# Loading the rows of three image pairs as bf16 with a casting DMA, in a convolution with max pooling

## The chip, the cores and the metric

The kernel runs on one core of a Trainium2 chip. A core has a matrix engine (TensorE, "PE" in the profile), three engines that work elementwise (VectorE or "DVE", ScalarE or "ACT", GpSimd or "POOL") and a synchronisation engine ("SP") that here only issues transfers. Each engine runs its own list of instructions in order; semaphores tie the lists together. SBUF is the core's working memory. PSUM, eight banks of 128 x 512 float32 here, takes the matrix engine's results; DVE and ACT read and write it, POOL does not in this kernel.

The metric is the time of one execution on the device in microseconds (us), the median of several runs. The times within a trace are counted from the start of its span.

## What is computed

A 3 x 3 convolution of 16 images with 64 channels of 64 x 64 to 128 channels, with a border of zeros, followed by the maximum over every 2 x 2 block:

```python
batch, c_in, h, w, c_out, k = 16, 64, 64, 64, 128, 3
x_pad = np.pad(x, ((0, 0), (0, 0), (pad, pad), (pad, pad)), mode='constant')
conv[b, co] += weight[co, ci, kh, kw] * x_pad[b, ci, kh:kh+h, kw:kw+w]   # for all b, co, ci, kh, kw
output[b, c, i, j] = np.max(conv[b, c, 2*i:2*i+2, 2*j:2*j+2])
```

Input and output are float32; the products are made in bf16 and summed in float32.

## The kernel before

**Tiling.** Two images form a pair: their 2 x 64 channels fill the 128 partitions, image 0 in the lower and image 1 in the upper half. A pair is cut into four quarters of 16 rows (R = 8 rows of the pooled result). There are eight pairs, so 32 steps, numbered 0 to 31. A step makes, for each of its two images l = 0 and 1, two banks: bank A and bank B, which together stand for the even and the odd rows of the convolution. A product is three matrix multiplications (one for each column of the 3 x 3 window) of 64 channels by 8 rows x 64 columns; the two images' products run side by side on the two halves of the array.

**Two kinds of steps.** The string SEQ gives each step a kind. The eight "K" steps (pairs 0 and 1) multiply the rows themselves, five products for an image. The 24 "W" steps (pairs 2 to 7, four steps each) save one: the vertical part of the window is rewritten so that four products are enough, at the price of sums and differences of rows that other engines make first. For a W step s these are:

- E.s: difference of neighbouring rows (128 x 512 elements), read by product P2
- S.s: sum of neighbouring rows (128 x 512), read by product P1
- V.s: difference of rows two apart (128 x 1024), read by P0 and P3; in a few steps made as two halves Ve.s and Vo.s

Each is written as bf16 (tiles we, ws, wv, vh) from rows that lie in SBUF as float32 (tiles wx). K steps have a similar sum, KS.s (tile ks), of rows that are bf16 already (tiles kx).

**Who makes them.** The suffix in the written order names the engine: `:v` DVE, `:g` POOL. POOL makes all V of the later steps and part of E and S. DVE makes the rest. The helper row_op (L195 to L200) issues them, and keeps note of the last one that DVE made through it (last_row): the next one on POOL waits for that one by a semaphore. For eleven steps a copy "CP.s:bank" (function lift, L287) first brings one of the two row operands into a PSUM bank, on ACT. Then DVE's E.s and S.s read one operand from PSUM and one from SBUF (two_rows, L294), and are not noted in last_row.

**Loads.** W rows come by SP's queue, one DMA for each quarter (LX.s, L262), with a row of overlap, into one of four float32 tiles wx (pair p uses wx[p % 4]; each has a zero row at top and bottom that POOL clears at the start, L150 to L152). Each such load waits until step s - 12 is finished (function paced). K rows of the later steps come by POOL's queue with a cast to bf16 (LK.s, L275).

**After the products.** ACT moves bank A to SBUF (EV, L429) and copies it as a start value into bank B (SE, L445; three of them on DVE, L443); DVE takes the larger of the two rows in bank B (MX, L449); ACT copies the odd columns out (OD, L472), DVE takes the larger of the columns (CM, L481), and SP stores the result (ST, L504). A bank is free for the next step's product or copy after EV or CM.

**The order.** The string ORDER (L16 to L80) lists every operation of every engine by hand; each engine works through its own entries in that order. A name such as P2.25.1:7 is product P2 of step 25, image 1, into bank 7. Entries that the change touches stand among these lines (L46 to L70). For POOL and DVE, the entries of steps 17 to 31 that matter here come in this order (CP on ACT and LX left out): S.16:v, V.16:g, S.15:g, E.17:v, E.19:g, S.17:v, V.17:g, S.19:g, E.22:v, S.22:v, V.22:g, KS.23:v, LK.27, E.20:v, V.19:g, E.21:g, V.20:g, S.20:v, V.21:g, S.21:g, E.24:g, V.24:g, S.24:v, KS.27:v, E.26:g, V.25:g, E.25:v, S.25:v, V.26:g, E.29:g, S.26:g, S.29:g, E.28:v, V.28:g, V.29:g, Ve.30:g, Ve.31:g, Vo.30:g, E.31:g, S.28:v, E.30:v, S.30:v, Vo.31:g, S.31:g.

Of the kernel before, what the change touches and what calls it, by code (L numbers as in the profile page):

```python
# [42 lines left out]
LX.19 OD.11.0 MX.12.0 P3.13.1 PBa.14.0:7 EV.13.1 LX.20 P2.13.0:6 P0.12.1 LX.22 CM.11.0 PBb.14.0  # L43
P2.15.1:0 S.16:v SE.13.0:2 MX.13.1 EV.12.1 SE.15.1:5 LK.23 P3.12.1 P1.12.0 OD.12.0 MX.14.0 ST.6
MX.12.1 P1.13.1 P0.13.0 OD.13.1 ST.2 P3.13.0 P0.15.1 CM.12.0 CM.13.1 EV.13.0 P3.15.1 P2.16.0:3
MX.13.0 EV.15.1 PR.14.0 PBa.14.1:6 CP.17:1 V.16:g S.15:g P1.13.0 P1.12.1 MX.15.1 SE.16.0:0 OD.14.0  # L46
E.17:v E.19:g CM.14.0 S.17:v OD.12.1 ST.4 OD.13.0 CM.12.1 P0.16.0 PBb.14.1 MX.14.1 V.17:g EV.16.0
ST.7 ST.9 P2.15.0:7 P1.15.1 LX.21 OD.15.1 P3.16.0 P2.16.1:1 S.19:g SE.15.0:3 P0.15.0 PR.14.1 CM.15.1
CM.13.0 CP.22:4 SE.16.1:5 OD.14.1 MX.16.0 P3.15.0 P2.17.1:2 P1.16.0 P0.16.1 EV.15.0 SE.17.1:7 E.22:v
OD.16.0 CM.14.1 MX.15.0 EV.16.1 P2.17.0:6 P3.16.1 P0.17.1 P1.15.0 SE.17.0:1 S.22:v CM.16.0 LX.24  # L50
P3.17.1 PAa.18.0:4 V.22:g PAa.18.1:0 P0.17.0 OD.15.0 MX.16.1 KS.23:v P1.16.1 PAb.18.0 EV.17.1 LK.27
CM.15.0 CP.20:2 P3.17.0 PBa.18.1:3 EV.17.0 MX.17.1 E.20:v OD.16.1 MX.17.0 V.19:g PAb.18.1 PBa.18.0:6
EV.18.0 P2.19.0:4 PBb.18.1 E.21:g EV.18.1 V.20:g P1.17.0 P1.17.1 ST.8 LX.26 CM.16.1 SE.19.0:5
MX.18.1 S.20:v OD.17.0 CM.17.0 P2.19.1:0 PBb.18.0 OD.17.1 SE.19.1:2 MX.18.0 P0.19.0 PR.18.1 OD.18.1
P2.22.1:1 P3.19.0 P0.19.1 PR.18.0 EV.19.0 CM.17.1 SE.22.1:7 OD.18.0 ST.11 P3.19.1 P2.20.0:4 EV.19.1
# [3 lines left out]
CM.22.1 EV.21.0 EV.21.1 MX.21.0 P3.21.1 P2.22.0:4 MX.21.1 SE.22.0:2 P1.20.0 P2.20.1:7 P2.24.1:0  # L59
P1.21.0 LX.29 ST.14 ST.12 OD.20.0 SE.20.1:6 CM.20.0 OD.21.0 CM.21.0 P0.22.0 P1.21.1 SE.24.1:3 ST.13  # L60
S.24:v EV.22.0 P0.20.1 P3.22.0 OD.21.1 KS.27:v CM.21.1 EV.20.1 P0.24.1 PAa.23.0:1 MX.22.0 E.26:g
P2.24.0:4 P3.24.1 EV.24.1 CP.25:7 V.25:g MX.24.1 PAb.23.0 PAa.23.1:5 SE.24.0:0 P1.22.0 P3.20.1
E.25:v EV.23.0 P1.24.1 P0.24.0 OD.24.1 S.25:v EV.24.0 P2.25.1:1 P3.24.0 MX.20.1 P2.25.0:7 PAb.23.1
LX.31 ST.17 P1.20.1 PBa.23.0:4 CM.24.1 OD.22.0 MX.24.0 SE.25.1:3 CM.22.0 EV.23.1 V.26:g SEv.25.0:2
P1.24.0 P0.25.1 OD.20.1 OD.24.0 EV.25.1 LX.30 ST.18 ST.22 ST.19 ST.21 PBb.23.0 P2.26.1:5 CM.20.1
ST.20 CM.24.0 ST.24 MX.23.0 SE.26.1:6 P3.25.1 P0.25.0 P3.25.0 PBa.23.1:0 EV.25.0 PR.23.0 P0.26.1
MX.25.1 P2.26.0:1 PBb.23.1 MX.25.0 E.29:g CP.28:7 S.26:g S.29:g E.28:v OD.23.0 P3.26.1 P1.25.0
V.28:g V.29:g CM.23.0 MX.23.1 Ve.30:g EV.26.1 P1.25.1 PAa.27.0:5 SE.26.0:4 PR.23.1 P0.26.0 MX.26.1
Ve.31:g P3.26.0 P1.26.1 Vo.30:g E.31:g OD.25.0 OD.25.1 EV.26.0 CM.25.0 S.28:v PAa.27.1:2 PAb.27.0
CP.30:7 CM.25.1 ST.25 MX.26.0 OD.23.1 P2.28.1:1 PBa.27.0:3 OD.26.1 PAb.27.1 P1.26.0 EV.27.0 CM.23.1  # L70
ST.23 PBb.27.0 PBa.27.1:0 CM.26.1 E.30:v SE.28.1:5 S.30:v Vo.31:g P0.28.1 P2.29.0:6 MX.27.0
P2.28.0:7 PBb.27.1 PR.27.0 P3.28.1 EV.27.1 OD.26.0 CM.26.0 ST.26 SE.29.0:2 MX.27.1 EV.28.1 OD.27.0
P2.29.1:4 P0.29.0 P3.29.0 PR.27.1 SE.28.0:1 EV.29.0 CM.27.0 MX.28.1 P0.28.0 P2.30.1:3 MX.29.0
# [10 lines left out]
def kernel(  # L84
# [14 lines left out]
    B, CI, H, W = x.shape  # L99
# [4 lines left out]
    R = HO // NQ  # L104
# [3 lines left out]
    const = ctx.enter_context(tc.tile_pool(name="const", bufs=1))  # L108
# [28 lines left out]

    def chunk(s):

        p, q = place[s]  # L140
        same = any(place[t] == (p, q - 1) and SEQ[t] == SEQ[s] for t in range(N))
        lo = 2 * R * q + 1 if same else max(0, 2 * R * q - 1)
        return p, lo, min(H, 2 * R * (q + 1) + 1)

    def half(s):
        return 2 * R * place[s][1] + R + 1

    NWX = 4
    wx = [const.tile([128, H + 2, W], FP32, name=f"wx_{i}") for i in range(NWX)]
    for t in wx:  # L150
        nc.gpsimd.memset(t[:, 0, :], 0.0)
        nc.gpsimd.memset(t[:, H + 1, :], 0.0)  # L152
    kx = {}

    def kx_of(p):
        if p not in kx:
            kx[p] = kx_pool.tile([128, H, W], BF16, name="kx")
        return kx[p]
# [10 lines left out]
    make_identity(nc, ident)  # L169
    zeros = const.tile([128, 512], BF16)  # L170
    begun = nc.gpsimd.memset(zeros, 0.0)
    wv = wraw.rearrange("a (c k) -> a k c", k=K * K)

    def ring(t, k):
# [20 lines left out]
    def row_op(e, out, in0, in1, op):  # L195
        inst = eng[e].tensor_tensor(out=out, in0=in0, in1=in1, op=op)  # L196
        if e == "g":
            behind(inst, last_row[0])
        else:
            last_row[0] = inst  # L200
# [50 lines left out]
    def paced(s, inst):  # L251

        for l in (0, 1):
            behind(inst, done.get((s - AHEAD[SEQ[s]], l)))
        if SEQ[s] == "K" and s < AHEAD["K"] and s not in kf:
            behind(inst, done["head"])

    def load(s, part, e):
        p, lo, hi = chunk(s)
        if SEQ[s] == "W":  # L260
            t = wx[p % NWX]
            paced(s, nc.sync.dma_start(out=t[:, lo + 1 : hi + 1, :], in_=rows_of(p, lo, hi)))  # L262
            return
        if s not in kf:
            kf[s] = const.tile([128, hi - lo, W], FP32, name=f"kf_{s}")
        a, b = {"": (lo, hi), "a": (lo, half(s)), "b": (half(s), hi)}[part]
        q = nc.scalar if e == "a" else nc.sync
        inst = q.dma_start(out=kf[s][:, a - lo : b - lo, :], in_=rows_of(p, a, b))
        paced(s, inst)
        if e == "a":  # L270
            behind(inst, begun)
# [15 lines left out]
    def lift(s, bank):  # L287

        lifted[s] = acc[bank]
        nc.scalar.copy(out=acc[bank], in_=wrow(s, 0))  # L290

    def two_rows(s, t, e, op):
        if e == "v" and s in lifted:
            nc.vector.tensor_tensor(out=t, in0=lifted[s], in1=wrow(s, 1), op=op)  # L294
        else:
            row_op(e, t, wrow(s, 0), wrow(s, 1), op)

    def wrow(s, a):

        p, q = place[s]  # L300
        f = 2 * R * q + a + 1
        return wx[p % NWX][:, f : f + 2 * R - 1 : 2, :]

    def ks(s, e):
        p, q = place[s]
# [8 lines left out]
    def rs_add(s):  # L314
# [23 lines left out]
    def rv(s, e):  # L338
        p, q = place[s]
        t = row["V", s] = v_pool.tile([128, 2 * R, W], BF16, name="wv")  # L340
        f = 2 * R * q
        u = wx[p % NWX]
        row_op(e, t, u[:, f + 2 : f + 2 + 2 * R, :], u[:, f : f + 2 * R, :], SUB)

    def rv_half(s, e, odd):

        p, q = place[s]
        t = row["V" + "eo"[odd], s] = vh_pool.tile([128, R, W], BF16, name="vh")
        f = 2 * R * q + odd
        u = wx[p % NWX]  # L350
        row_op(e, t, u[:, f + 2 : f + 1 + 2 * R : 2, :], u[:, f : f + 2 * R - 1 : 2, :], SUB)


# [168 lines left out]
    for token in ORDER.split():  # L522
        what, _, at = token.partition(":")
        name, *args = what.split(".")
        if name in PRODUCTS:
            s, l = int(args[0]), int(args[1][0])
# [87 lines left out]
```

## Time and profile before

| what | value |
|---|---|
| median of 3 runs | 103.27 us (103.05 to 103.55) |
| span of the profiled execution | 101.5 us |
| DMA packets | 13789, 24.07 MB |
| read from and written to HBM | 17.07 MB, 8.39 MB |

The page states the span of the profiled execution, from its first to its last instruction, and no total for it; the runs' times also hold what lies before and after the span.

How to read the rows: "L196" is line 196 of the kernel. A group names line, engine, operation, tile written and tiles read, their sizes (partitions x elements, type) and the number of instructions, then busy time, mean duration in ns, and the engine's idle time just before them with what ended it. Since one helper line makes many operations, the tile's name tells which: we, ws, wv, vh for E, S, V and the halves of V. "PEld" is the loading of weights. An engine's idle time costs something only where the engine is late for another.

The page's share of busy time in 40 equal slices of the span, in tenths:

```profile
PE   6999999999999999999989999999999999999950
...
DVE  0599999999999999799999989998999999888980
ACT  5599999999988999998999989989989889899840
POOL 7000898988598599989999999998599999999000
...
DMA  2999999991079989889998999999953915302353
```

All four computing engines are busy most of the time from about 10 us on.

### The profile page before, as it was taken

How to read it: one execution, taken by the hardware profiler on the slowest of the kernel's cores; microseconds unless marked ns; L12 is line 12 of the kernel's file. 1: busy time of each engine (PE TensorE's matmuls, PEld its weight loads, DVE VectorE, ACT ScalarE, POOL GpSimd, SP SyncE). 2: the span in 40 equal slices, each digit the busy share in tenths (PEclk: the TensorE clock that was granted, in tenths of full speed). 3: DMA queues.
4: the chain of work that ended last, by engine and by line, in shares of the span. 5: the costliest groups of instructions: out<-in, count | busy, mean ns of one | idle time of the engine just before them, and what ended most of it. 6: DMA issues, size and time to landing. Idle time of an engine off the chain costs nothing.

```text
span 101.5 us, 2486 instructions
## 1 busy us (share of the span) xinstructions
PE 96.4 (95%) x870; PEld 55.6 (55%) x870; DVE 91.4 (90%) x181; ACT 89.5 (88%) x198; POOL 79.3 (78%) x65
## 2 busy tenths in 40 slices
PE   6999999999999999999989999999999999999950
PEld 2356885466666666555645555455475555655510
DVE  0599999999999999799999989998999999888980
ACT  5599999999988999998999989989989889899840
POOL 7000898988598599989999999998599999999000
PEclk9999999999999999999999999999999999999999
DMA  2999999991079989889998999999953915302353
GB/s 45 328 248 403 417 376 337 326 226 33 6 203 390 233 166 302 315 222 291 273 329 260 261 237 311 374 392 308 295 222 122 344 58 201 108 29 78 110 189 121
DMA packets 13789, 24.07 MB, mean 237 GB/s; under 512 B 1104, under 2 KB 9680, under 8 KB 13776
## 3 DMA queue, kind: packets, MB, share of 16 engines
q1 hardware_dynamic: 12624, 22.16, 64.9%
q0 software_dynamic: 864, 1.56, 10.2%
q10 hardware_dynamic: 288, 0.20, 0.6%
q8 instruction: 7, 0.11, 0.4%
q14 instruction: 6, 0.05, 0.1%
HBM read 17.07 MB, written 8.39 MB: 251 GB/s over the span
## 4 chain that ended last, share of the span: by engine, by line
PE 83%; ACT 6%; DVE 3%; DMA 3%; issue 2%; DVEq 0%; ACTq 0%
PE acc L414 80%; DMA wraw<-in_weight_dram 3%; ACT acc L445 3%; PE acc L229 2%; DVE acc L449 2%; ACT od L472 2%; ACT ev L429 1%; DVE o L481 1%; ACT wq L191 1%; DVE acc L443 0%; PE acc L439 0%; DVEq L609 0%; DVEq L449 0%; DVEq L443 0%; ACTq L290 0%
## 5 line engine op out<-in xcount | busy, mean ns | idle before, releaser
L414 PEld LDWEIGHTS <-wt 64*128 64x128 bf16 x840 | 52.8, 94 | 37.3 <-issue 2.5
L414 PE MATMUL acc<-wv,wt 64*128 64x504 bf16 (+1 forms) x228 | 49.5, 377 | 0.3 <-ACT acc L445 0.3
L449 DVE TENSOR_TENSOR acc<-acc,ev 128x512 f32<-128x512 f32 x64 | 42.9, 693 | 2.0 <-ACT ev L429 1.1
L196 POOL TENSOR_TENSOR wv<-wx 128x1024 bf16<-128x1024 f32 x18 | 42.3, 2362 | 2.5 <-DVE ks L196 1.6
L414 PE MATMUL acc<-kx,wt 64*128 64x504 bf16 (+6 forms) x216 | 38.9, 350 | 0.0
L414 PE MATMUL acc<-ws,wt 64*128 64x512 bf16 (+1 forms) x144 | 35.2, 377 | 0.2 <-DVE acc L449 0.2
L414 PE MATMUL acc<-we,wt 64*128 64x512 bf16 (+1 forms) x144 | 35.1, 377 | 0.0
L429 ACT ACTIVATE ev<-acc 128x512 f32<-128x512 f32 x48 | 28.6, 610 | 1.1 <-PE acc L414 1.0
L445 ACT COPY acc<-acc 128x512 f32<-128x512 f32 x45 | 26.3, 588 | 2.0 <-PE acc L414 0.4
L481 DVE TENSOR_TENSOR o<-acc,od 128x256 f32<-128x256 f32 (+1 forms) x65 | 25.7, 412 | 1.4 <-ACT od L472 0.5
L472 ACT COPY od<-acc 128x256 f32<-128x256 f32 x64 | 23.6, 382 | 2.7 <-PE acc L414 1.9
L196 POOL TENSOR_TENSOR we<-wx 128x512 bf16<-128x512 f32 x11 | 14.0, 1272 | 2.8 <-DVE ks L196 1.7
L414 PE MATMUL acc<-ks,wt 64*128 64x504 bf16 (+1 forms) x48 | 12.5, 377 | 0.0
L414 PE MATMUL acc<-vh,wt 64*128 64x504 bf16 (+1 forms) x60 | 10.4, 376 | 0.0
L196 POOL TENSOR_TENSOR ws<-wx 128x512 bf16<-128x512 f32 x8 | 10.1, 1268 | 0.1
L275 POOL DMA_DIRECT2D kx<-in_x_dram x6 | 3.5, 590 | 8.0 <-ACT ev L429 8.0
L431 ACT COPY ev<-acc 128x512 f32<-128x512 f32 x16 | 9.3, 598 | 0.4 <-PE acc L414 0.3
L196 POOL TENSOR_TENSOR vh<-wx 128x512 bf16<-128x512 f32 x7 | 8.8, 1272 | 0.5 <-DVE ks L196 0.4
L294 DVE TENSOR_TENSOR we<-acc,wx 128x512 bf16<-128x512 f32 x11 | 7.5, 682 | 0.0
L294 DVE TENSOR_TENSOR ws<-acc,wx 128x512 bf16<-128x512 f32 x11 | 7.5, 681 | 0.0
L290 ACT COPY acc<-wx 128x512 f32<-128x512 f32 x11 | 6.7, 607 | 0.1
L509 PE MATMUL acc<-const-bfloat16-1.0 128*128 128x512 bf16 x8 | 3.6, 625 | 0.8 <-PEq L595 0.8
(30 smaller groups left out, 34.3 us busy)
## 6 DMA issues: line engine op xcount, KB each, us to landing
out_dram<-o SPq DMA_DIRECT2D x30, 256.0 KB, 5.8
wx<-in_x_dram SPq DMA_DIRECT2D x12, 512.0 KB, 6.3
wx<-in_x_dram SPq DMA_DIRECT2D x6, 544.0 KB, 6.5
wx<-in_x_dram SPq DMA_DIRECT2D x6, 480.0 KB, 6.7
kx<-in_x_dram POOLq DMA_DIRECT2D x3, 256.0 KB, 7.2
kf<-in_x_dram SPq DMA_DIRECT2D x1, 512.0 KB, 7.7
kx<-in_x_dram POOLq DMA_DIRECT2D x2, 240.0 KB, 5.6
wraw<-in_weight_dram SPq DMA_DIRECT2D x1, 288.0 KB, 3.0
```

The costliest lines, as they stand in the source:

```text
L196: inst = eng[e].tensor_tensor(out=out, in0=in0, in1=in1, op=op)
L275: paced(s, nc.gpsimd.dma_start(out=kx_of(p)[:, lo:hi, :], in_=rows_of(p, lo, hi)))
L290: nc.scalar.copy(out=acc[bank], in_=wrow(s, 0))
L294: nc.vector.tensor_tensor(out=t, in0=lifted[s], in1=wrow(s, 1), op=op)
L414: yield lambda kw=kw, o0=o0, o1=o1, c0=c0, c1=c1: nc.tensor.matmul(acc[t][:, i0:i1, o0:o1], wt[l * CI : l * CI + CI, K * BLOCKS[block] + T ...
L429: inst = nc.scalar.mul(t, acc[bank["A", s, l]], -1.0)
L431: inst = nc.scalar.copy(out=t, in_=acc[bank["A", s, l]])
L445: nc.scalar.copy(out=acc[b], in_=acc[bank["A", s, l]])
L449: nc.vector.tensor_tensor(out=t, in0=t, in1=ev[s, l], op=MAX)
L472: nc.scalar.copy(out=od[s, l][:, i0:i1], in_=acc[bank["B", s, l]][:, i0:i1, 1::2])
L481: done[s, l] = nc.vector.tensor_tensor(out=outs(s)[:, l, i0:i1], in0=acc[bank["B", s, l]][:, i0:i1, 0::2], in1=od[s, l][:, i0:i1], op=MAX,)
L509: nc.tensor.matmul(acc[n], ones[:, 0:128], ones, start=True, stop=True, skip_group_check=True)
```

## The change

Pairs 5, 6 and 7 (steps 17, 19, 20, 21; 22, 24, 25, 26; 28 to 31) get bf16 tiles hx of their own in place of the shared float32 tiles, of which three remain for pairs 2 to 4. Their rows are loaded by POOL's queue with a cast, two quarters in one DMA: the entries LX.17, LX.20, LX.22, LX.25, LX.28 and LX.30 issue one each, at their old places in ORDER, now in POOL's list, and LX.19, LX.21, LX.24, LX.26, LX.29 and LX.31 issue nothing. These loads don't wait for an earlier step. The copies CP.17, CP.22, CP.20, CP.25, CP.28 and CP.30 go. E and S of these six steps thereby no longer read PSUM: they go through row_op, with both operands in hx. All other E, S and V of the three pairs read hx too. The border rows of the three new tiles are cleared on POOL, after the clearing of zeros. The rest of ORDER is as it was.

```diff
-MX.13.0 EV.15.1 PR.14.0 PBa.14.1:6 CP.17:1 V.16:g S.15:g P1.13.0 P1.12.1 MX.15.1 SE.16.0:0 OD.14.0
+MX.13.0 EV.15.1 PR.14.0 PBa.14.1:6 V.16:g S.15:g P1.13.0 P1.12.1 MX.15.1 SE.16.0:0 OD.14.0
...
-CM.13.0 CP.22:4 SE.16.1:5 OD.14.1 MX.16.0 P3.15.0 P2.17.1:2 P1.16.0 P0.16.1 EV.15.0 SE.17.1:7 E.22:v
+CM.13.0 SE.16.1:5 OD.14.1 MX.16.0 P3.15.0 P2.17.1:2 P1.16.0 P0.16.1 EV.15.0 SE.17.1:7 E.22:v
...
-    NWX = 4
+    NWX = 3
     wx = [const.tile([128, H + 2, W], FP32, name=f"wx_{i}") for i in range(NWX)]
...
+    HALVES = (B // 2 - 3, B // 2 - 2, B // 2 - 1)
+    hx = {p: const.tile([128, H + 2, W], BF16, name=f"hx_{p}") for p in HALVES}
+
+    def wx_of(p):
+        return hx[p] if p in hx else wx[p % NWX]
...
     begun = nc.gpsimd.memset(zeros, 0.0)
+    for t in hx.values():
+        nc.gpsimd.memset(t[:, 0, :], 0.0)
+        nc.gpsimd.memset(t[:, H + 1, :], 0.0)
...
         if SEQ[s] == "W":
-            t = wx[p % NWX]
+            t = wx_of(p)
+            if p in hx:
+                if place[s][1] % 2:
+                    return
+                hi = chunk(kinds["W"][kinds["W"].index(s) + 1])[2]
+                nc.gpsimd.dma_start(out=t[:, lo + 1 : hi + 1, :], in_=rows_of(p, lo, hi))
+                return
             paced(s, nc.sync.dma_start(out=t[:, lo + 1 : hi + 1, :], in_=rows_of(p, lo, hi)))
             return
...
-        return wx[p % NWX][:, f : f + 2 * R - 1 : 2, :]
+        return wx_of(p)[:, f : f + 2 * R - 1 : 2, :]
```

CP.20, CP.25, CP.28 and CP.30 are taken out of ORDER in the same way, and rv and rv_half (the makers of V, Ve and Vo) take their rows from wx_of(p).

More of the change, by code (lines that the diff above doesn't have):

```diff
@@ L45 @@
 MX.12.1 P1.13.1 P0.13.0 OD.13.1 ST.2 P3.13.0 P0.15.1 CM.12.0 CM.13.1 EV.13.0 P3.15.1 P2.16.0:3
-MX.13.0 EV.15.1 PR.14.0 PBa.14.1:6 CP.17:1 V.16:g S.15:g P1.13.0 P1.12.1 MX.15.1 SE.16.0:0 OD.14.0
+MX.13.0 EV.15.1 PR.14.0 PBa.14.1:6 V.16:g S.15:g P1.13.0 P1.12.1 MX.15.1 SE.16.0:0 OD.14.0
 E.17:v E.19:g CM.14.0 S.17:v OD.12.1 ST.4 OD.13.0 CM.12.1 P0.16.0 PBb.14.1 MX.14.1 V.17:g EV.16.0
 ST.7 ST.9 P2.15.0:7 P1.15.1 LX.21 OD.15.1 P3.16.0 P2.16.1:1 S.19:g SE.15.0:3 P0.15.0 PR.14.1 CM.15.1
-CM.13.0 CP.22:4 SE.16.1:5 OD.14.1 MX.16.0 P3.15.0 P2.17.1:2 P1.16.0 P0.16.1 EV.15.0 SE.17.1:7 E.22:v
+CM.13.0 SE.16.1:5 OD.14.1 MX.16.0 P3.15.0 P2.17.1:2 P1.16.0 P0.16.1 EV.15.0 SE.17.1:7 E.22:v
 OD.16.0 CM.14.1 MX.15.0 EV.16.1 P2.17.0:6 P3.16.1 P0.17.1 P1.15.0 SE.17.0:1 S.22:v CM.16.0 LX.24
 P3.17.1 PAa.18.0:4 V.22:g PAa.18.1:0 P0.17.0 OD.15.0 MX.16.1 KS.23:v P1.16.1 PAb.18.0 EV.17.1 LK.27
-CM.15.0 CP.20:2 P3.17.0 PBa.18.1:3 EV.17.0 MX.17.1 E.20:v OD.16.1 MX.17.0 V.19:g PAb.18.1 PBa.18.0:6
+CM.15.0 P3.17.0 PBa.18.1:3 EV.17.0 MX.17.1 E.20:v OD.16.1 MX.17.0 V.19:g PAb.18.1 PBa.18.0:6
 EV.18.0 P2.19.0:4 PBb.18.1 E.21:g EV.18.1 V.20:g P1.17.0 P1.17.1 ST.8 LX.26 CM.16.1 SE.19.0:5
@@ L61 @@
 S.24:v EV.22.0 P0.20.1 P3.22.0 OD.21.1 KS.27:v CM.21.1 EV.20.1 P0.24.1 PAa.23.0:1 MX.22.0 E.26:g
-P2.24.0:4 P3.24.1 EV.24.1 CP.25:7 V.25:g MX.24.1 PAb.23.0 PAa.23.1:5 SE.24.0:0 P1.22.0 P3.20.1
+P2.24.0:4 P3.24.1 EV.24.1 V.25:g MX.24.1 PAb.23.0 PAa.23.1:5 SE.24.0:0 P1.22.0 P3.20.1
 E.25:v EV.23.0 P1.24.1 P0.24.0 OD.24.1 S.25:v EV.24.0 P2.25.1:1 P3.24.0 MX.20.1 P2.25.0:7 PAb.23.1
@@ L66 @@
 ST.20 CM.24.0 ST.24 MX.23.0 SE.26.1:6 P3.25.1 P0.25.0 P3.25.0 PBa.23.1:0 EV.25.0 PR.23.0 P0.26.1
-MX.25.1 P2.26.0:1 PBb.23.1 MX.25.0 E.29:g CP.28:7 S.26:g S.29:g E.28:v OD.23.0 P3.26.1 P1.25.0
+MX.25.1 P2.26.0:1 PBb.23.1 MX.25.0 E.29:g S.26:g S.29:g E.28:v OD.23.0 P3.26.1 P1.25.0
 V.28:g V.29:g CM.23.0 MX.23.1 Ve.30:g EV.26.1 P1.25.1 PAa.27.0:5 SE.26.0:4 PR.23.1 P0.26.0 MX.26.1
 Ve.31:g P3.26.0 P1.26.1 Vo.30:g E.31:g OD.25.0 OD.25.1 EV.26.0 CM.25.0 S.28:v PAa.27.1:2 PAb.27.0
-CP.30:7 CM.25.1 ST.25 MX.26.0 OD.23.1 P2.28.1:1 PBa.27.0:3 OD.26.1 PAb.27.1 P1.26.0 EV.27.0 CM.23.1
+ CM.25.1 ST.25 MX.26.0 OD.23.1 P2.28.1:1 PBa.27.0:3 OD.26.1 PAb.27.1 P1.26.0 EV.27.0 CM.23.1
 ST.23 PBb.27.0 PBa.27.1:0 CM.26.1 E.30:v SE.28.1:5 S.30:v Vo.31:g P0.28.1 P2.29.0:6 MX.27.0
@@ L341, in rv @@
         f = 2 * R * q
-        u = wx[p % NWX]
+        u = wx_of(p)
         row_op(e, t, u[:, f + 2 : f + 2 + 2 * R, :], u[:, f : f + 2 * R, :], SUB)
@@ L349, in rv_half @@
         f = 2 * R * q + odd
-        u = wx[p % NWX]
+        u = wx_of(p)
         row_op(e, t, u[:, f + 2 : f + 1 + 2 * R : 2, :], u[:, f : f + 2 * R - 1 : 2, :], SUB)
```

## The prediction

> **What bounds the kernel now.** I read the page's busy times first, then the chain of work that ended last, then two stretches in which each engine's busy time is set against the length of the stretch. (Page; chain in order of time; stretches, whose columns are start:end, length, busy time and instructions of each engine, granted clock, DMA share, GB/s.)
>
> ```profile
> span 101.5 us, 2486 instructions
> PE 96.4 (95%) x870; PEld 55.6 (55%) x870; DVE 91.4 (90%) x181; ACT 89.5 (88%) x198; POOL 79.3 (78%) x65
> ...
> PE 83%; ACT 6%; DVE 3%; DMA 3%; issue 2%; DVEq 0%; ACTq 0%
> ```
> ```profile
> 53.10 34.67 PE acc L414 x316
> ```
> ```profile
> 46.50:93.80 47.30, 47.00 (x434) 25.57 (x432) 44.70 (x88) 44.46 (x100) 45.81 (x28) 1.00 0.76 237
> 88.00:97.00 9.00, 8.79 (x79) 4.94 (x76) 8.14 (x16) 8.39 (x20) 5.79 (x5) 1.00 0.32 107
> ```
>
> TensorE sets the end: the chain runs through its products without a break for 34.67 us, at full clock. But POOL's 78% is an average that hides what matters here. From 46.5 to 93.8 us, where nearly all of the change lies, POOL is busy 45.8 of 47.3 us and has 1.5 us to spare. DVE is busy 44.7. So anything added to POOL or taken from DVE there can become the new bound, unless the products have their operands well ahead of time. They have not. (Timelines of POOL and of TensorE: start, duration, what; in brackets the idle time before and what ended it.)
>
> ```profile
> 28.11 2.37 POOL L196 TENSOR_TENSOR wv<-wx 128x1024 bf16<-128x1024 f32 x1 [1.23 <-DVE ks L196]
> ...
> 39.52 4.67 POOL L196 TENSOR_TENSOR wv<-wx 128x1024 bf16<-128x1024 f32 x2
> ...
> 46.58 2.35 POOL L196 TENSOR_TENSOR wv<-wx 128x1024 bf16<-128x1024 f32 x1 [0.23 <-DVE ws L196]
> ...
> 54.90 2.37 POOL L196 TENSOR_TENSOR wv<-wx 128x1024 bf16<-128x1024 f32 x1
> ...
> 65.99 1.26 POOL L196 TENSOR_TENSOR ws<-wx 128x512 bf16<-128x512 f32 x1
> ...
> 72.17 1.28 POOL L196 TENSOR_TENSOR we<-wx 128x512 bf16<-128x512 f32 x1 [1.38 <-DVE ks L196]
> 73.40 4.68 POOL L196 TENSOR_TENSOR wv<-wx 128x1024 bf16<-128x1024 f32 x2
> ...
> 81.74 4.68 POOL L196 TENSOR_TENSOR wv<-wx 128x1024 bf16<-128x1024 f32 x2
> ...
> 90.07 1.27 POOL L196 TENSOR_TENSOR we<-wx 128x512 bf16<-128x512 f32 x1
> ...
> 92.52 1.27 POOL L196 TENSOR_TENSOR ws<-wx 128x512 bf16<-128x512 f32 x1
> ```
> ```profile
> 76.59 0.39 PE L414 MATMUL acc<-wv,wt 64*128 64x512 bf16 x1
> ...
> 92.08 0.83 PE L414 MATMUL acc<-we,wt 64*128 64x512 bf16 x6
> ...
> 96.44 1.40 PE L414 MATMUL acc<-ws,wt 64*128 64x512 bf16 x6 [0.21 <-DVE acc L449]
> ```
>
> Counting along the written order, the row at 73.40 holds V.25 and V.26; V.25 ends at about 75.78, and its first product starts at 76.59: a lead of 0.8 us. E.31 (90.07 to 91.34) leads by 0.74, S.31 (92.52 to 93.79) by 2.65.
>
> **What stands between DVE and POOL.** The rows of DVE's ks, a sum of two bf16 operands that both lie in SBUF, tell most. (DVE's timeline; then two lines' durations as minimum/median/maximum in ns.)
>
> ```profile
> 27.61 0.42 DVE L196 TENSOR_TENSOR ks<-kx 128x512 bf16<-128x512 bf16 x1
> ...
> 30.14 0.62 DVE L196 TENSOR_TENSOR ks<-kx 128x512 bf16<-128x512 bf16 x1
> ...
> 43.91 0.57 DVE L196 TENSOR_TENSOR ks<-kx 128x512 bf16<-128x512 bf16 x1
> ...
> 57.03 0.52 DVE L196 TENSOR_TENSOR ks<-kx 128x512 bf16<-128x512 bf16 x1
> ...
> 73.66 0.68 DVE L294 TENSOR_TENSOR we<-acc,wx 128x512 bf16<-128x512 f32 x1
> ...
> 82.55 0.68 DVE L294 TENSOR_TENSOR ws<-acc,wx 128x512 bf16<-128x512 f32 x1
> ```
> ```profile
> L196 DVE TENSOR_TENSOR ks<-kx x8: 415/443/622, 10.1 to 71.7; 128x512 bf16<-128x512 bf16 x8
> ```
> ```profile
> L294 DVE TENSOR_TENSOR we<-acc,wx x11: 677/681/691, 11.7 to 84.9; 128x512 bf16<-128x512 f32 x11
> L294 DVE TENSOR_TENSOR ws<-acc,wx x11: 680/681/683, 12.3 to 85.5; 128x512 bf16<-128x512 f32 x11
> ```
>
> Three of them start while a POOL instruction runs, and each ends 0.28 to 0.29 us after it: POOL ends at 30.48, 44.19 and 57.27; ks ends at 30.76, 44.48 and 57.55. With 0.42 us for a free one (27.61), they got going 0.13 us ahead of POOL's end, whatever their start. So a DVE instruction with both operands in SBUF waits until POOL's running instruction is nearly over. The lifted form, one operand in PSUM, never varies: 677 to 691 ns over 22, though most of them lie inside POOL instructions (73.66 inside 73.40 to 75.78). The copy into PSUM keeps these two engines apart.
>
> **The change part by part.**
>
> ```profile
> L290 ACT COPY acc<-wx 128x512 f32<-128x512 f32 x11 | 6.7, 607 | 0.1
> L275 POOL DMA_DIRECT2D kx<-in_x_dram x6 | 3.5, 590 | 8.0 <-ACT ev L429 8.0
> L196 POOL TENSOR_TENSOR wv<-wx 128x1024 bf16<-128x1024 f32 x18 | 42.3, 2362 | 2.5 <-DVE ks L196 1.6 <-DVE we L196 0.7 <-DVE ws L196 0.2
> L196 POOL TENSOR_TENSOR we<-wx 128x512 bf16<-128x512 f32 x11 | 14.0, 1272 | 2.8 <-DVE ks L196 1.7 <-DVE ws L196 1.0
> ```
>
> 1. Six copies leave ACT: 6 x 0.607 = 3.6 us. ACT is not the bound; they count nothing for the end. They lie beside products; at most they undo the 0.5 us that TensorE stands in the two stretches above (0.30 and 0.21). Their banks come free earlier, at the same price.
>
> 2. Twelve sums and differences (E and S of steps 17, 20, 22, 25, 28, 30) turn from one PSUM operand at 0.68 us to two bf16 operands in SBUF, the form of ks, at 0.42: DVE gains 12 x 0.26 = 3.1 us. S.24 gains as much once. In exchange each now contends with POOL in both directions. DVE waits for POOL's running instruction: with the times as they are, E.25 (73.66) would wait to 75.65, 2.0 us, and S.28 (82.55), inside the V.28 and V.29 that follow each other from 81.74 to 86.42, 1.4 us. And the later POOL row operations get a semaphore on them, since the helper that makes them notes the last DVE row operation; the lifted form wasn't noted. Behind a waiting POOL instruction all its later work queues, its DMA issues too, and behind those the products; behind a waiting DVE sum queue the row and column maxima that free the banks. For POOL's side I count one handover of 0.42 us for each of the twelve: 5.0 us. Lower bound 0, if each falls into a DMA issue or a wait of POOL's own; upper bound, POOL waits for DVE to come by, which cost it up to 1.38 us in a row above (72.17): eight of its instructions (E.19, V.17, V.22, V.19, V.21, V.26, V.28, Vo.31) stand directly behind one of the twelve or a pair of them, 8 x 1.38 = 11.0. I take 5.0, since DVE and POOL are within a microsecond or two of each other. DVE's waits and POOL's are two sides of the same handovers, so I add one side only.
>
> 3. Twelve loads leave SP, which nothing waits for, and six issues come onto POOL at 0.58 us (the row's mean is 0.59 with the first, longer one), one packet for a partition as now, so no longer. Four (17, 20, 22, 30) simply delay POOL: 2.3 us. Of that 0.2 goes into the wait ahead of 46.58; rest 2.1. The paced waits of SP's loads go too, but POOL comes by later than SP did, so no load starts earlier than its data is wanted; the landings of 17, 20, 22 and 30 have over 8 us each and I cost them at nothing.
>
> 4. The loads of 25 and 28 stand right behind S.21 (65.99) on POOL, and E.26 needs the third and fourth quarter of that pair, which is the load of 25. Only E.24 and V.24 lie between. (Two casting loads issued together; then all six.)
>
> ```profile
> 17.75 1.11 POOL L275 DMA_DIRECT2D kx<-in_x_dram  x2
> ```
> ```profile
> kx<-in_x_dram POOLq DMA_DIRECT2D x1, 240.0 KB, 5.2
> ```
> ```profile
> kx<-in_x_dram POOLq DMA_DIRECT2D x1, 272.0 KB, 6.0
> ```
> ```profile
> DMA to landing us min/median/max: 5.2/6.6/7.9
> ```
>
> The first of the two landed at 22.95, the second at 18.32 + 6.0 = 24.3: 1.4 us for the same amount again. A load of twice the rows then lands 6.6 us after its issue at the least (5.2 + 1.4) and 8.0 by the median; I take 7.0, near the two that were issued behind each other, as these are. Before, 4.9 us lay between S.21's end (67.25) and E.26 (72.17), 1.38 of it waiting for ks. So E.26 comes 7.0 - 4.9 = 2.1 us later (1.7 to 3.1), in which the two issues and ks's wait are contained. E.25 on DVE waits for the same landing. The Trainium skill, "DMA: Bandwidth & Descriptors", section "Anatomy of one DMA — SWDGE (gpsimd) path", fits 2.0 us plus the bytes at 436 GB/s. As an estimate by that page, 1 MB would land 4.4 us after the 0.58 us issue, E.26 would be held for 0.1 us instead of 2.1, and the sum would be 2 us less; the rows, 5.2 us for half as much, say otherwise.
>
> 5. Six more clears of one border row on POOL and two fewer, ahead of its 8 us idle wait (the L275 row's idle time): nothing.
>
> Sum on POOL: 2.1 + 2.1 + 5.0 = 9.2 us. The lead takes some of it: by S.31 (2.65) 6.6 us remain, by E.31 (0.74) 8.5. Near the end ACT and DVE, freed of 3.6 and 3.1 us, can make up part of what E.31 loses, so I take 6.9, close to S.31's. Against the profiled span that is 101.5 + 6.9 = 108.4. The page gives no total for its own execution; the runs' median, 103.27, lies 1.8 us above the span, so 110.2 us.
>
> **The rivals.** (a) Handovers cost nothing, because the twelve fall where POOL waits or issues. Then 4.2 us are left on POOL, less a lead of 0.7 to 2.65: 1.6 to 3.5, about 105.8 us. For it: 1.5 us of idle time and 3.5 us of new issues are there to be hit. Against it: twelve meetings, and POOL running 45.8 of 47.3 us.
>
> (b) Waits in both directions: POOL stands at the semaphore until a late DVE comes, then DVE at POOL. The upper bound, 11.0 in place of 5.0, gives 116.2 us. For it: DVE, too, has little idle time (44.7 of 47.3), and the banks that it frees are wanted at once.
>
> (c) Not slower: POOL's instructions become shorter because they read bf16. DVE's do so, 415 against 681 ns. Twenty-five of POOL's read the new tiles, ten wide and fifteen half: 10 x 2.362 + 15 x 1.272 = 42.7 us. From 6.9 / 42.7 = 16% shorter (the wide one under 1.98 us) the added work is paid. At DVE's ratio of 0.61 they would save 16.7 us, POOL would be no bound, and the 0.5 us of TensorE's standing would go: 102.7 us. No row shows POOL reading two bf16 operands, so the bounds are 0 and that. Against it: DVE reads the f32 form slower by itself, whereas POOL's 2.13 ns for each further element ((2362 - 1272) / 512) is far over the 0.81 ns that DVE takes in all (415 / 512), which looks like its own work and not the width of what it reads. The Trainium skill, "GPSIMD Engine Reference", section "Elementwise — side-by-side cycle accounting", has about 2.6 cycles for an element of two inputs, taken one after the other, and speaks of elements, not of bytes; by that page there would be no gain, and the row agrees as far as f32 goes.
>
> (d) The change doesn't do what it says: a casting load of twice the rows takes twice the descriptors, and POOL issues for 1.15 us instead of 0.58: 3.5 us more, 113.7 us. Against it: six loads of 15 to 17 rows all took 538 to 699 ns only, which can't tell.
>
> **How the numbers follow.** Forecast 62%, (a) 16%, (b) 9%, (c) 9%, (d) 4%. The time is 110.2 us. The forecast's own range, from the bounds of landing and lead with handovers of 3 to 7 us, is 107.5 to 113.2. To hold 8 in 10 the range has to take in most of (a) and the edge of (d): 104.8 to 113.7. About 0.5% is what a measurement of this kernel can tell from no change. Of (c), half is faster by over 0.5 us and a third within it; a little of (a) falls within it as well: faster 0.05, same 0.04, slower 0.91.
>
> **What would show it.** Right: the twelve at L196 on DVE with durations spread from 0.42 to over 2 us, many ending 0.28 us after a POOL instruction; POOL idle behind DVE's we and ws; a wait of POOL or DVE for hx's landing near E.26; TensorE waiting for wv and we. Wrong: all twelve at 0.42 us (then (a)); POOL's wide instruction well under 2.36 us (then (c)); issues of over 1 us (then (d)); or TensorE still without gaps.

## The result, and the profile after

The changed kernel takes 110.44 us (median of 4 runs, 109.91 to 111.12) against 103.41 us (103.05 to 103.78) for the kernel before on the same chip: 1.0674 times as long, 95% interval 1.0618 to 1.0731. Ratios, here and below, leave out disturbed runs, in which the granted clock was lower and the time longer; the traces of e1, e5 and e6 are of such runs (113.38, 108.43 and 111.38 us), and their ratios are a little smaller than the medians give.

The page of the changed kernel, its first two lines:

```profile
span 108.4 us, 2467 instructions
PE 98.8 (91%) x870; PEld 54.1 (50%) x870; DVE 96.1 (89%) x181; ACT 87.1 (80%) x192; POOL 80.0 (74%) x75
```

The span grew by 6.9 us. POOL is not busier for it: 80.0 us against 79.3, with six more DMA issues in it. ACT is busy 2.4 us less, without the six copies, and DVE, whose twelve sums were to become shorter, is busy 4.7 us longer. The groups of line 204 (the old line 196) say why, with the new loads in the last row; columns as before.

```profile
L204 POOL TENSOR_TENSOR wv<-hx 128x1024 bf16<-128x1024 bf16 x10 | 21.4, 2144 | 3.4 <-DVE ws L204 1.7 <-DVE we L204 1.2 <-PE acc L428 0.5
L204 POOL TENSOR_TENSOR wv<-wx 128x1024 bf16<-128x1024 f32 x8 | 18.9, 2364 | 2.3 <-DVE ks L204 1.6 <-DVE we L204 0.7
...
L204 POOL TENSOR_TENSOR we<-hx 128x512 bf16<-128x512 bf16 x6 | 7.1, 1186 | 1.7 <-DMA hx<-in_x_dram 1.3 <-DVE we L204 0.4
L204 POOL TENSOR_TENSOR we<-wx 128x512 bf16<-128x512 f32 x5 | 6.3, 1268 | 1.4 <-DVE ws L204 1.0 <-DVE ks L204 0.4
L204 DVE TENSOR_TENSOR we<-hx 128x512 bf16<-128x512 bf16 x6 | 6.2, 1029 | 0.0
...
L204 DVE TENSOR_TENSOR ks<-kx 128x512 bf16<-128x512 bf16 x8 | 5.7, 718 | 0.0
L204 DVE TENSOR_TENSOR ws<-hx 128x512 bf16<-128x512 bf16 x7 | 5.6, 805 | 0.0
...
L274 POOL DMA_DIRECT2D hx<-in_x_dram x6 | 3.4, 560 | 0.0
```

Three things stand there. DVE's E and S on the new tiles should take 0.42 us and take 1.03 and 0.81 in the mean: 11.8 us for thirteen (S.24 among them) where 5.4 would do, so 6.4 us of waiting counted as busy. KS, which nobody edited, has gone from 481 to 718 ns. And POOL's instructions on bf16 are shorter than those on float32 next to them: 2144 against 2364, 1186 against 1268 ns.

The place that cost most is E.25, which comes just in time for its product. DVE, POOL and TensorE in their timelines:

```profile
77.17 2.15 DVE L204 TENSOR_TENSOR we<-hx 128x512 bf16<-128x512 bf16 x1
79.25 0.41 DVE L204 TENSOR_TENSOR ws<-hx 128x512 bf16<-128x512 bf16 x1
...
85.03 1.12 DVE L204 TENSOR_TENSOR we<-hx 128x512 bf16<-128x512 bf16 x1
```
```profile
75.81 1.16 POOL L204 TENSOR_TENSOR we<-hx 128x512 bf16<-128x512 bf16 x1 [1.27 <-DMA hx<-in_x_dram]
76.91 2.13 POOL L204 TENSOR_TENSOR wv<-hx 128x1024 bf16<-128x1024 bf16 x1
79.83 2.13 POOL L204 TENSOR_TENSOR wv<-hx 128x1024 bf16<-128x1024 bf16 x1 [0.79 <-DVE ws L204]
...
83.61 2.25 POOL L204 TENSOR_TENSOR ws<-hx 128x512 bf16<-128x512 bf16 x2
...
96.61 1.16 POOL L204 TENSOR_TENSOR ws<-hx 128x512 bf16<-128x512 bf16 x1
```
```profile
79.38 0.39 PE L428 MATMUL acc<-we,wt 64*128 64x512 bf16 x1 [1.24 <-DVE we L204]
```
```profile
102.49 0.39 PE L428 MATMUL acc<-ws,wt 64*128 64x512 bf16 x1 [0.22 <-DVE acc L463]
```

E.26 (75.81) waited 1.27 us for its rows to land. V.25 began at 76.91, E.25 on DVE at 77.17 and ended at 79.32: 0.28 us after V.25's end, as the three KS rows of before had it. TensorE stood 1.24 us for it, and POOL then 0.79 us for S.25. The same meeting shows at 85.03 (E.28 ends 0.29 us after S.29, which ends at 85.86). But look at the end. S.31, POOL's last, ends at 97.77, 4.0 us later than before, while its product starts at 102.49, 6.05 us later: POOL's lead there has grown from 2.65 to 4.72 us. In the last stretch POOL was not what TensorE waited for; DVE was.

Following the first product of each step through both traces, the delay is 0.1 us up to P2.11 and grows in jumps. Each jump but two stands behind a DVE instruction of line 204 with a wait in it: to 0.5 us at 47.8 (behind KS.18, 1.17 us long), 1.1 at 52.4 (E.17, 1.31), 1.4 at 54.5 (S.17, 1.26), 2.2 at 60.5 (KS.23, 1.78), 4.9 at 79.4 (E.25, 2.15), 5.4 at 87.2 (E.28, 1.12), 6.1 at 93.0 (S.30, 1.37). The two others, 2.4 at V.21 (69.2) and 3.2 at E.24 (72.5), are POOL being late.

The rest came after all computing. DVE's last work ends with the last row of the chain (first the changed kernel, then the kernel before):

```profile
104.62 0.20 DVEq L623
```
```profile
98.58 0.20 DVEq L609
```

From 104.82 to the end of the span are 3.55 us. In the trace of before the same point is at 98.78, 2.72 us ahead of the end. So 6.04 us were lost in the work and 0.83 in the closing.

### The profile page after: what moved, and what is told of

The parts are those of the page before. It is cut to its first block, busy times and chain, and to the rows that moved or that the text cites. A ratio compares the mean times of both kernels' runs of the same rounds, so it can differ in the third digit from the quotient of the medians.

```text
span 108.4 us, 2467 instructions
## 1 busy us (share of the span) xinstructions
PE 98.8 (91%) x870; PEld 54.1 (50%) x870; DVE 96.1 (89%) x181; ACT 87.1 (80%) x192; POOL 80.0 (74%) x75
## 5 line engine op out<-in xcount | busy, mean ns | idle before, releaser
L428 PEld LDWEIGHTS <-wt 64*128 64x128 bf16 x840 | 51.3, 94 | 45.0 <-issue 8.6
L428 PE MATMUL acc<-wv,wt 64*128 64x504 bf16 (+1 forms) x228 | 50.9, 377 | 0.4 <-ACT acc L459 0.3
L204 POOL TENSOR_TENSOR wv<-hx 128x1024 bf16<-128x1024 bf16 x10 | 21.4, 2144 | 3.4 <-DVE ws L204 1.7
L204 POOL TENSOR_TENSOR wv<-wx 128x1024 bf16<-128x1024 f32 x8 | 18.9, 2364 | 2.3 <-DVE ks L204 1.6
L204 POOL TENSOR_TENSOR we<-hx 128x512 bf16<-128x512 bf16 x6 | 7.1, 1186 | 1.7 <-DMA hx<-in_x_dram 1.3
L204 POOL TENSOR_TENSOR we<-wx 128x512 bf16<-128x512 f32 x5 | 6.3, 1268 | 1.4 <-DVE ws L204 1.0
L204 DVE TENSOR_TENSOR we<-hx 128x512 bf16<-128x512 bf16 x6 | 6.2, 1029 | 0.0
L204 POOL TENSOR_TENSOR ws<-hx 128x512 bf16<-128x512 bf16 x5 | 6.0, 1199 | 0.0
L204 DVE TENSOR_TENSOR ks<-kx 128x512 bf16<-128x512 bf16 x8 | 5.7, 718 | 0.0
L204 DVE TENSOR_TENSOR ws<-hx 128x512 bf16<-128x512 bf16 x7 | 5.6, 805 | 0.0
```

The source lines that it names most:

```text
L428: yield lambda kw=kw, o0=o0, o1=o1, c0=c0, c1=c1: nc.tensor.matmul(acc[t][:, i0:i1, o0:o1], wt[l * CI : l * CI + CI, K * BLOCKS[block] + T ...
```

## The experiments

All ratios are against the kernel before, run on the same chip between the runs of the experiment.

| kernel | casting loads | copies | ratio (95% interval) | median, us |
|---|---|---|---|---|
| changed kernel | as changed | dropped | 1.0674 (1.0618 to 1.0731) | 110.44 |
| e1 | as changed | all back | 1.0592 (1.0525 to 1.0659) | 109.95 |
| e2 | none, float32 loads on SP | dropped | 1.0898 (1.0864 to 1.0932) | 112.91 |
| e3 | load of 25 earlier | dropped | 1.0579 (1.0526 to 1.0632) | 109.80 |
| e4 | as changed | dropped, not noted | 1.2192 (1.2121 to 1.2262) | 126.40 |
| e5 | all early | all back | 1.0354 (1.0298 to 1.0410) | 107.92 |
| e6 | all early | dropped | 1.0654 (1.0612 to 1.0696) | 110.30 |
| e7 | all early | back but for step 25 | 1.0459 (1.0392 to 1.0527) | 107.91 |
| e8 | spread | all back | 1.0116 (1.0086 to 1.0145) | 104.74 |
| e9 | spread | dropped | 1.0383 (1.0353 to 1.0413) | 107.47 |
| e10 | as e8, four more transfers on SP | all back | 1.0071 (1.0047 to 1.0095) | 104.19 |
| e11 | kernel before, four more transfers on SP | as before | 1.0017 (1.0001 to 1.0033) | 103.54 |

### e1, the copies back

```diff
-MX.13.0 EV.15.1 PR.14.0 PBa.14.1:6 V.16:g S.15:g P1.13.0 P1.12.1 MX.15.1 SE.16.0:0 OD.14.0
+MX.13.0 EV.15.1 PR.14.0 PBa.14.1:6 CP.17:1 V.16:g S.15:g P1.13.0 P1.12.1 MX.15.1 SE.16.0:0 OD.14.0
...
```

(the same for CP.22, CP.20, CP.25, CP.28 and CP.30, at their old places)

> The changed kernel with the six copies into PSUM put back, now from the bf16 tiles; the casting loads stay. Theory, the handovers between DVE and POOL cost most: they are gone, what is left are the issues (2.1 us) and the landing (2.1 us) less POOL's shorter instructions (the ten wide ones 2144 against 2364 ns, 2.2 us, and about 1 us from the half ones), so 103.5 to 105.5 us, and no DVE instruction of these steps over 0.75 us. Rival, POOL's own work (issues and landing) sets the end: it stays at 108 to 110.5 us. Rival, the bf16 operands in themselves are the harm: 110 us.

Measured 1.0592: hardly better. That is above the range of 103.5 to 105.5 us, and by the number alone the rivals would have won. The waits of the profiled execution show another thing (engine, what waited, for whom: us in total, times, longest):

```profile
ACT acc L304 <- DMA hx<-in_x_dram: 5.8, 2, 3.2
DVE o L495 <- ACT od L486: 4.6, 6, 3.2
POOL we L204 <- PE acc L428: 3.9, 1, 3.9
```

The copies now read the tiles that the casting loads fill. Their place in ACT's list had been chosen for loads that SP, in the trace of before, issued 4 to 14 us earlier; so ACT, with all of its bank traffic behind it, stood 5.8 us at two copies for the landing. The experiment had exchanged one wait for another, and told the two causes apart only in that all twelve sums took 678 to 692 ns again, none of them held by POOL. In this trace two stands of TensorE (2.03 and 2.46 us) also come with 3.4 us each at half the granted clock. To separate them, the loads had to be moved as well (e5 on).

### e2, the copies dropped and nothing else

```diff
-MX.13.0 EV.15.1 PR.14.0 PBa.14.1:6 CP.17:1 V.16:g S.15:g P1.13.0 P1.12.1 MX.15.1 SE.16.0:0 OD.14.0
+MX.13.0 EV.15.1 PR.14.0 PBa.14.1:6 V.16:g S.15:g P1.13.0 P1.12.1 MX.15.1 SE.16.0:0 OD.14.0
...
```

> The kernel before with nothing but the six copies dropped: float32 tiles and SP's loads stay, and E and S of the six steps read two float32 operands in SBUF. Theory, handovers: as slow as the changed kernel or slower, since each of the twelve takes 0.68 us with the pair of ports instead of 0.42 and POOL's instructions keep their 2.36 us: 109 to 113 us. Rival, issues and landing of the casting loads: these are not here, so 103 to 105 us.

Measured 1.0898, 9.4 us: as the theory has it, and slower than the changed kernel, without any casting load of W rows. DVE's sums in the trace (minimum/median/maximum; 683 ns if free):

```profile
L196 DVE TENSOR_TENSOR ws<-wx x11: 679/823/1749, 9.1 to 94.4; 128x512 bf16<-128x512 f32 x11
...
L196 DVE TENSOR_TENSOR we<-wx x8: 674/816/2755, 5.9 to 93.3; 128x512 bf16<-128x512 f32 x8
```

So dropping the copies is a loss by itself, and the bf16 tiles gave part of it back.

### e3, one load earlier

```diff
-S.21:g LX.25 OD.19.0 EV.22.1 P2.21.1:6 P0.20.0 SE.21.0:1 CM.19.0 LX.28 E.24:g ST.16 EV.20.0 MX.22.1
+S.21:g OD.19.0 EV.22.1 P2.21.1:6 P0.20.0 SE.21.0:1 CM.19.0 LX.28 E.24:g ST.16 EV.20.0 MX.22.1
```

(and LX.25 behind LK.27 instead)

> The changed kernel with one casting load, that of steps 25 and 26, issued right behind the load of step 27, some 10 us earlier. Theory: POOL's wait for its landing (1.27 us ahead of E.26) goes, and E.25 meets POOL elsewhere; as DVE's wait for POOL at E.25 (2.15 us) came right behind, only 0.5 to 2 us are won: 108.5 to 110 us. Rival, landing decides that stretch: 2.1 us or more are won, 107.5 to 108.3 us. Rival, the landing was covered: 110.4 us, the same.

Measured 1.0579, about 1% or 1 us less than the changed kernel, though the two intervals just overlap: within the theory's range, and the landing wait at E.26 is gone from the trace (0.71 us for KS.27 stand in its place). What stood behind it is the meeting at E.25, which is still there: E.25 takes 1.59 us instead of 2.15.

### e4, the twelve not noted

```diff
         else:
+            noted = last_row[0]
             row_op(e, t, wrow(s, 0), wrow(s, 1), op)
+            if s in (17, 20, 22, 25, 28, 30):
+                last_row[0] = noted if e == "v" else last_row[0]
```

> The changed kernel, but the twelve E and S on DVE are not noted as the last row operation, so that POOL's later row operations don't wait for them by a semaphore. Theory, the contention itself (DVE waits until POOL's running instruction is nearly over, and a POOL instruction that starts under a DVE one is held too) is what costs: 108.5 to 112 us, DVE's we and ws with longer durations than the 1029 and 805 ns of the changed kernel, as POOL now always has an instruction running. Rival, the semaphore waits of POOL (5.1 us of idle time ahead of rows on hx) are the loss: 105 to 107 us.

Measured 1.2192. The direction was the theory's, the size was outside all that was expected. One DVE instruction and POOL's list beside it:

```profile
92.56 9.34 DVE L204 TENSOR_TENSOR we<-hx 128x512 bf16<-128x512 bf16 x1
```
```profile
90.80 4.20 POOL L204 TENSOR_TENSOR wv<-hx 128x1024 bf16<-128x1024 bf16 x2
94.97 3.34 POOL L204 TENSOR_TENSOR vh<-hx 128x512 bf16<-128x512 bf16 x3
98.27 1.13 POOL L204 TENSOR_TENSOR we<-hx 128x512 bf16<-128x512 bf16 x1
99.38 1.14 POOL L204 TENSOR_TENSOR vh<-hx 128x512 bf16<-128x512 bf16 x1
100.48 1.13 POOL L204 TENSOR_TENSOR ws<-hx 128x512 bf16<-128x512 bf16 x1
```

DVE waited 9.3 us, through eight POOL instructions that followed each other without a gap, and ended at 101.90, 0.29 us after the last. It was not let in between them; E.17, at 52.35, was held for 5.57 us in the same way. But that is not always so: in the same trace E.20, S.20 and E.25 (1.60, 1.93 and 1.57 us long) ended 0.28 to 0.29 us after one POOL instruction while the next one of POOL's stood right behind it. So the semaphore that I had counted as a second cost bounds DVE's wait: where POOL stops for it, DVE gets its turn at the latest. It does not rid DVE of waiting for the POOL instructions ahead of that stop. Nor are the 16 us more than in the changed kernel DVE's waits alone: TensorE stood for 4.62 and 8.40 us, and around these stands the granted clock was half for 3.4 and 6.8 us.

### e5, e6, e7: the loads early

```diff
-... V.10:g E.10:g MX.4.1 ...
+... V.10:g E.10:g LX.17 LX.20 MX.4.1 ...
-EV.8.0 LK.18 S.12:v ...
+EV.8.0 LK.18 LX.22 LX.25 S.12:v ...
-V.15:g MX.11.0 ...
+V.15:g LX.28 MX.11.0 ...
-... OD.22.1 V.24:g CM.19.1
+... OD.22.1 V.24:g LX.30 CM.19.1
```

(the old places of the six entries are empty; e5 has all six copies, e6 none, e7 all but CP.25)

> The changed kernel with the six copies put back, and each of the six casting loads moved to an earlier place in POOL's list, where POOL stood waiting in the trace of before (17 and 20 behind E.10, 22 and 25 behind the load of 18, 28 behind V.15, 30 behind V.24). Theory, two causes that cover each other, the handovers and the late landing (with the copies back alone, ACT's copies waited 5.8 us for the landings): both are gone here, so 102.5 to 104.5 us, no wait for hx, and all twelve DVE sums at 0.68 us. Rival, something else in the casting loads costs (their packets, POOL's time to issue, DVE reading bf16 beside PSUM): 106 to 109 us.

> The same early casting loads, with the six copies dropped as in the changed kernel. Theory: the handovers are left alone to act, and cost by themselves most of the slowdown: 107 to 109.5 us, DVE's we and ws on hx still over 0.41 us in most of the twelve and up to 2 us, no wait for hx. Rival, late landing and issues set the changed kernel's time and the handovers little: 103 to 105 us.

> As the one with early loads and all copies, but with the copy of step 25 alone dropped: E.25 and S.25 read both operands in SBUF beside POOL's V.25. Theory: DVE's E.25 arrives inside V.25 and waits up to 2.1 us for it, and P2.25 stands right behind E.25 (0.2 us of lead before): 1 to 2.5 us more than with all six copies. Rival, DVE makes up a single wait and the 0.5 us that two shorter sums and a missing copy save count: within 0.5 us of it.

Measured 1.0354, 1.0654 and 1.0459. The first missed its range, with a time inside the rival's, and the second came out at 110.30 us, 0.8 above its own. The trace of e5 says where its time went. Two stretches of it (columns as in the prediction):

```profile
39.00:50.00 11.00, 9.03 (x68) 3.90 (x66) 6.66 (x13) 8.24 (x18) 7.85 (x6) 0.84 1.07 291
50.00:96.00 46.00, 45.70 (x422) 24.80 (x420) 43.36 (x87) 42.77 (x97) 42.58 (x30) 1.00 0.56 151
```

In this trace TensorE loses 4.4 us, all by 47 us, and none after. The two loads at 27 us had filled the transfer engines just when the float32 rows of steps 13, 15 and 16 were due (ACT's copy of step 13 waited 2.8 us for them, POOL's E.15 2.1 us). TensorE stood for 1.92 us up to 41.77, and shortly behind, from 43.33 on, the granted clock was half for 3.4 us (the 0.84 of the first row). That second part is not in every execution: e7, with the same loads, stood for 1.82 us at the same place and has no such stretch, and its trace had lost only 2.6 us by 47 us. From 50 us on TensorE is busy 45.7 of 46.0 us: with the copies back and the rows there in time, nothing in the changed stretch costs anything. That part of the theory holds; that early is better was wrong as such.

The three share the early loads, so their differences count. Without the copies (e6 against e5): 3.0% or 3.1 us; both traces have the stretch at half clock, and TensorE ends 2.9 us later in e6's. Without the copy of step 25 alone (e7 against e5): 1.05% or 1.1 us, with intervals that overlap, so this one rests on e7's trace: the delay there is nearly flat from 43 us on (2.5 to 2.6 us) but for one jump of 1.1 us, at the product behind E.25, which POOL held for 1.4 us:

```profile
78.12 0.39 PE L428 MATMUL acc<-we,wt 64*128 64x512 bf16 x1 [0.79 <-DVE we L204]
```

### e8 and e9: the loads spread

```diff
-EV.8.0 LK.18 S.12:v ...
+EV.8.0 LK.18 LX.17 LX.20 S.12:v ...
-V.15:g MX.11.0 ...
+V.15:g LX.22 MX.11.0 ...
```

(and LX.25 behind LK.27, LX.28 behind V.20, LX.30 behind V.24; e8 with the copies, e9 without)

> All six copies back, and the casting loads early but spread: 17 and 20 behind the load of step 18, 22 behind V.15, 25 behind the load of step 27, 28 behind V.20, 30 behind V.24. With the loads of 17 and 20 at 27 us the transfers of steps 13, 15 and 16 came late and all lost 4 us by 43 us, and nothing after that. Theory: without that collision and with the copies there is nothing left that costs: 102.7 to 104.3 us. Rival, casting loads cost wherever they stand, by taking the transfer engines from others: 105.5 us or more.

> The same spread loads with the six copies dropped. Theory: the handovers alone, which in the two kernels with early loads made the delay grow by 2.9 us from 47 us on (and by 1.1 us at E.25 alone), cost 3 to 5.5 us: 106 to 109 us, against the one with the copies. Rival, what DVE and ACT save pays for them: within 1 us of the one with the copies.

Measured 1.0116 and 1.0383: 104.74 us, 0.4 us above the range expected, and 107.47, inside. The pair gives the price of the handovers best: 2.7 us, net of what the quicker sums and the missing copies save. DVE's sums on hx in e8, and in e9:

```profile
L308 DVE TENSOR_TENSOR we<-acc,hx x6: 679/686/692, 50.4 to 85.3; 128x512 bf16<-128x512 f32 x6
L308 DVE TENSOR_TENSOR ws<-acc,hx x6: 677/680/681, 51.3 to 85.9; 128x512 bf16<-128x512 f32 x6
```
```profile
L204 DVE TENSOR_TENSOR ws<-hx x7: 411/657/1370, 51.2 to 88.2; 128x512 bf16<-128x512 bf16 x7
L204 DVE TENSOR_TENSOR we<-hx x6: 408/497/1580, 50.4 to 87.5; 128x512 bf16<-128x512 bf16 x6
```

In e8 the slower form never varies, in e9 the quicker one goes up to 1.6 us. And from the changed kernel to e9 (1.0674 to 1.0383) nothing but the places of the six loads differs: 3.0 us. In e8's trace the computing ends only 0.48 us later than before, yet the span is 1.3 us longer: the closing again.

### e10 and e11: the closing

```diff
-            paced(s, nc.sync.dma_start(out=t[:, lo + 1 : hi + 1, :], in_=rows_of(p, lo, hi)))
+            cuts = (lo, 4, 8, 11, 14, hi) if s == 12 else (lo, hi)
+            for c, d in zip(cuts, cuts[1:]):
+                paced(s, nc.sync.dma_start(out=t[:, c + 1 : d + 1, :], in_=rows_of(p, c, d)))
```

> The kernel with all copies back and spread loads (104.74 us), with the load of step 12 cut into five, so four more transfers on SP at a quiet time. In its trace the last landing lies 1.69 us ahead of the end, in the trace of before 0.98; SP's closing waits stand in a fixed order of semaphores, and twelve transfers fewer put the last store on a semaphore that is waited for early in it. Theory: four more bring it back to the old place: 0.5 to 0.8 us less, 103.9 to 104.3 us, and about 1.0 us between last landing and end. Rival, the closing is long for another reason (the casting queue): 104.7 us, 1.7 us as before.

> The kernel before with the same load cut into five. Theory of the closing waits: the last store moves to the unlucky place, 0.5 to 0.8 us more than before, 103.9 to 104.3 us, with 1.7 us between last landing and end. Rival: 103.4 us as before, 1.0 us.

Measured 1.0071 (0.45% or 0.5 us less than e8, with intervals that overlap; 0.98 us from the last landing to the end, as in the trace of before) and 1.0017 (103.54 us, 0.14 more than before and below its range; 1.21 us from the last landing, not 1.7). So the number of transfers on SP does move the end, and four more undo the changed kernel's loss there. In the traces the last store signals semaphore 109 in the kernel before and in e10, and 103 in the changed kernel, e8 and e11, with five of SP's closing waits behind it instead of one: the move that the theory asked for did happen in e11, but it cost 0.2 us instead of 0.7. So the place of the last store's semaphore is not all of it; what else in the kernels with casting loads lengthens the closing stays open.

None of these beats the kernel before. The best, e10, has all of its copies and is 0.7% slower.

## Why the prediction was right

The time (110.2 us) and the span (108.4) came out almost to the digit. The terms did not: some were too large and others were missing, and they cancelled, so that the total fits so well is luck. By the pairs of runs, the 7.0 us are 3.0 for the places of the six loads, 2.7 net for the handovers, and the 1.2 that e8 still loses: 0.5 in the work, 0.8 in the closing.

**What bounds the kernel: right.** TensorE's list had no slack, POOL and DVE too little, and each late operand went into the end.

**Handovers, 5.0 us: right mechanism, too large.** The pair e9 and e8 measures 2.7 us, e6 and e5 3.1. The step that failed was to count POOL's side alone and let POOL set the end. POOL's last sum was to come 9.2 us later; it came only 4.0 us later and led by 4.72 us. Of the 6.0 us lost in the work, only the two jumps at V.21 and E.24, 1.0 us, stand behind POOL; the rest ran through DVE, by its waits at KS.18, E.17, S.17, KS.23, E.25, E.28 and S.30. The one at E.25, which the prediction had put at 2.0 us of DVE's time, held DVE for 1.7 us; in e7, where it held DVE for 1.4, it cost 1.1 us of the whole by itself. I also named the semaphore as a price; without it the kernel takes 126.40 us instead of 110.44 (e4).

**The bf16 gain, counted as DVE's 3.1 us and nothing on POOL: the second half failed.** POOL's wide instructions were 9% shorter and the half ones 2 to 7%, some of them lengthened by DVE; that is 3.1 us in all by the means of the groups (10 x 0.22, the fifteen others 0.9). That is part of rival (c), though short of the 16% at which it would have paid. With float32 tiles the same handovers cost 9.4 us (e2) instead of 2.7: DVE's shorter sums and POOL's would make up most of that difference, an account that I did not test piece by piece. The Trainium skill's rule for POOL, in "GPSIMD Engine Reference", section "Elementwise — side-by-side cycle accounting", that a two-input operation takes about 2.6 cycles for each element, would have had no gain at all; the rows differ from it by these 9%.

**Issues and the late landing, 4.2 us of POOL's time: near in sum, wrong in its parts.** What the places of the six loads cost together is 3.0 us (changed kernel against e9). The landing at E.26 was put at 2.1 us; E.26 came 5.57 us after S.21's end instead of 4.92, so 0.65 later:

```profile
hx<-in_x_dram POOLq DMA_DIRECT2D x1, 496.0 KB, 5.5
```

That load took 5.5 us, under my lowest bound of 6.6. The estimate by the Trainium skill, "DMA: Bandwidth & Descriptors", section "Anatomy of one DMA — SWDGE (gpsimd) path" (0.58 + 4.4 us), was nearer here; the other five took 6.7 to 8.6, far over it. More was lost where I counted only the issue time: LX.17 pushed V.15 under KS.18, whose wait rose from 0.16 to 0.75 us, and LX.20 and LX.22 pushed V.16 and S.15 under E.17. An issue on POOL does not only delay POOL; it moves every meeting behind it.

**Not foreseen: the closing, 0.83 us.** The prediction had no term for what follows the last computing, though it noted that twelve transfers leave SP.

**The rivals.** (a), handovers at no cost, fell with e2 and e9. (b), waits in both directions, is what happened in kind, but the two did not add up. (c) was right in sign and too small. (d) fell: an issue took 0.56 us for the double load.

## What to carry to other kernels

A copy that looks superfluous may be there to keep two engines off each other: before it is dropped, look at the durations of the operation that it feeds, and if they never vary while the same operation in another form does, the copy buys that. When work is moved to an engine that another one waits for, look up not only its length but which waits behind it slide into which running instruction, and where in its list each transfer's data is first touched. And when undoing one half of a change brings nothing, look whether the other half now acts in its place before calling it harmless.

## What the runs showed of the hardware that was not expected

- DVE, waiting with two SBUF operands, was held through eight POOL instructions in a row (9.3 us, e4). In the changed kernel it did get in between two of them, at S.20, S.28, E.30 and S.30, and POOL's following instruction was then longer, 1.32 to 1.33 us instead of 1.15, and 2.32 instead of 2.13 behind S.28. When it gets in and when not was not settled.
- One operand in PSUM, bf16 or float32 in SBUF: 677 to 692 ns in all rows of the kernel before, e1 and e8, whatever POOL did.
- POOL's sums on bf16 are shorter than on float32: 2119 against 2367 ns for the wide ones in e8, where nothing disturbs them, 1150 against 1270 for the others.
- A casting DMA of 0.5 MB written took POOL 0.54 to 0.58 us to issue, as one of half the size.
- Stands of TensorE of 1.92 (e5), 1.93 (e6), 2.03 and 2.46 (e1), 4.62 and 8.40 us (e4) each had a stretch of 3.4 or 6.8 us at half the granted clock in them or shortly behind; those of 1.82 us (e7) and 1.24 us (the changed kernel) had none. That is no sharp rule: at 7.5 us in e4 such a stretch follows a stand of only 0.95 us.
